# Seven half-K block products for 44 feature tiles, ahead of both branches, with narrower edge blocks in the attention

## The chip, the core and the metric

The kernel runs on one core of a Trainium2 chip. The metric is the device time of one execution in microseconds, as the median of several runs. TensorE (PE) multiplies matrices into the eight banks of PSUM, VectorE (DVE) and ScalarE (ACT) work elementwise and are the only engines here that read PSUM, GpSimd (POOL) does little, and SyncE (SP) issues nearly all transfers between device memory and the on-chip buffer from one queue, in order.

## What is computed

A hybrid encoder layer over two sequences, a prompt of 1024 tokens (s = 0) and a sample of 2048 (s = 1), each with 16 learned meta tokens ahead. All in float32.

```python
xn = _rmsnorm(h, g_pre)
proj = xn @ w_in + b_in                      # 1024 -> 6672 columns
na_q, na_k, na_v, na_z, ml_qk, ml_v, ml_z, ml_o, ml_g, mg = jnp.split(proj, SPLIT_IDX, axis=-1)
ya = _neighbourhood_attention(na_q, na_k, na_v, na_rpb)   # 8 heads of 64, windows of 8 rows x 16 columns of a 64 wide grid
ya = (ya * jax.nn.silu(na_z)) @ w_a
yb = (_mlstm_branch(ml_qk, ml_v, ml_g, ml_o, ml_conv_w, ml_head_g) * jax.nn.silu(ml_z)) @ w_b   # 4 heads of 128, both directions
ga, gb = jnp.split(jax.nn.sigmoid(mg), 2, axis=-1)
y = (ga * ya + gb * yb) @ w_out
return h + _rmsnorm(y, g_post)
```

## The kernel before

Every float32 operand of a large product is split into a rounded part (hi) and the rest (lo): ScalarE copies hi, VectorE subtracts to get lo. `mm3` then adds three products (hi hi, hi lo, lo hi) into one PSUM bank. A weight tile is loaded as `wraw`, split into `whi` and `wlo` (`wpump`, four buffers of each), and the split parts are written back to device memory for later use. The tokens are split into `xh` and `xl` (`build_half`, 512 tokens at a time).

There are two streams of work. The dense stream (`dense`) makes the projections and the final stage. A feature-major tile (`fm_half`) holds 128 columns of `proj` for 512 tokens: eight k tiles x three parts, 24 matmuls of 512 columns, into a `pj` bank, and then `fm_evac`. A token-major unit (`tm_unit`) takes 128 tokens x 256 columns. `PLAN` lists the order of the groups: sequence, first token and kinds of columns (m: for the mLSTM, n: for the attention, g: the merge gates, f: final blocks of 512 tokens, `final` and `final_out`). The sparse stream (`sparse`) makes the two branches: `ml` (gates, then for each head `ml_states` and `ml_outputs`, two chunks of 128 tokens at a time) and `na` (per head and block of eight rows, four units of 16 query columns each: `na_scores`, `na_scale`, `na_turn`, `na_out`).

`run` writes both streams into one program. The order on TensorE is as written: after each step of a branch, which names a length in microseconds (`A_D`, `A_A`, `A_NA`), dense matmuls of that length are put in. `STEPS` sets the order of the branches: mLSTM of the prompt, its attention, mLSTM of the sample, its attention. A branch starts when the groups that it needs have been written; until then the dense stream is alone. The order on the other engines is set when the program is built, by a scheduler that knows its own durations.

Names that the steps touch: `sc`, `tr` and `sm` are PSUM banks (one, two, two; `pj` has three). In `ml_outputs`, `um` is the decay tile of a pair of chunks, four buffers, loaded from `ud`; VectorE adds the mask `trim` (L1245), multiplies by the scores (L1279), and `sl` (L1286) is its last reader. `num` and `ccl` are the numerators and the low part of the state. In `na`, `prb` holds the probabilities of a unit, `pts` their transpose, `yg` the output of a head pair. `tg` are the merge gates in the final stage, `yh`, `yl`, `mh`, `mlo` its operands.

The attention's key columns: a unit reads 32 of the 64 grid columns, from `KC0`; the matmul count of a unit follows from that, a chunk of eight key columns at a time:

```python
KC0 = (0, 8, 24, 32)
    N, kc, g0 = ns * 32, KC0[cb], (5, 1, 0)[typ]
    for ch in range(4):
        nc.tensor.transpose(pt[:ks, ch, :], pr_[:, ch * ks:(ch + 1) * ks], self.ident)
```

Of the kernel before, what the change touches and what calls it, by code (L numbers as in the profile page):

```python
# [17 lines left out]
P = 128  # L18
# [3 lines left out]
NM = 16  # L22
# [18 lines left out]
PLAN = ((0, 0, "m"), (0, 0, "n"), (1, 0, "m"), (1, 1024, "m"), (1, 1024, "n"), (1, 0, "n"), (1, 0, "g"), (1, 1024, "g"), (0, 0, "g"), ("f", 0, 0), ("f", 0, 1), ("f", 1, 0), ("f", 1, 1), ("f", 1, 2), ("f", 1, 3))  # L41
STEPS = (("ml", 0, ()), ("na", 0, (0, 1)), ("ml", 1, ()), ("na", 1, (0, 1, 2, 3)))
KC0 = (0, 8, 24, 32)
OFFC = (15, 7, 7, -1)
# [27 lines left out]
def _consts():  # L72
# [9 lines left out]
    for typ, tl in ((0, 0), (1, 1), (2, R // 8 - 1)):  # L82
# [3 lines left out]
        for si, row in enumerate(slots):  # L86
            for c0 in range(49):
                m = np.full(64, NEG, np.float32)
                if row is None:
                    m[(8 if c0 < 24 else 32):][:NM] = 0.0  # L90
                else:
                    m[c0:c0 + 16] = 0.0
                masks[typ, c0, si] = m
# [27 lines left out]
class K:  # L121
# [3 lines left out]
    def __init__(self, tc, ins, outs):  # L125
# [7 lines left out]
        self.need = False  # L133
        self.hold, self.early = deque(), True
# [14 lines left out]

    def psum(self, tag, shape):  # L150
        return self.pp.tile(shape, F32, name=tag, tag=tag, bufs=BANKS[tag])

    def mm3(self, out, ah, al, bh, bl, start=True, stop=True):

        mm = self.nc.tensor.matmul
        mm(out, ah, bh, start=start, stop=False)  # L156
        mm(out, ah, bl, start=False, stop=False)  # L157
        mm(out, al, bh, start=False, stop=stop)  # L158
# [25 lines left out]
    def setup2(self):  # L184
# [5 lines left out]
        self.bq8 = cp.tile([P, 4], F32, name="bq8")  # L190
        nc.vector.tensor_scalar(self.bq8, self.bfm[:, 0:4], 0.125, None, op0=ALU.mult)
# [28 lines left out]
    def wload(self, most=2):  # L220

        while self.wreq and sum(x[1] is not None for x in self.wraw) < most:
            key, src, nk, w = self.wreq.popleft()
            raw = None
            if key not in self.wseen:
# [5 lines left out]
    def wpump(self, most=NBW, parts=1, copy=None):  # L231
# [4 lines left out]
        while self.wraw and self.wout < most:  # L236
# [4 lines left out]
            if raw is None:  # L241
# [153 lines left out]
    def build_half(self, s, t0, res):  # L395

        nc, wp = self.nc, self.wp
        if (s, t0) in self.xkept:
# [9 lines left out]
            return  # L408
        if s == 0:
# [55 lines left out]
    def xkeep(self, s, t0, x):  # L465
        where = [j for j, g in enumerate(PLAN) if g[:2] == (s, t0 // 1024 * 1024)]
        if where[-1] - where[0] >= len(where):
# [6 lines left out]
    def beside(self):  # L474

        self.turn += 1
        if self.xput and self.turn % 2:
# [3 lines left out]
    def fm_evac(self, col, s, t0, meta, chunks, ps):  # L481
# [7 lines left out]
        for (c0, c1), p in zip(chunks, ps):  # L489
# [6 lines left out]
            if col < C_NK:  # L496
                nc.scalar.activation(o.rearrange("p (b r c) -> p r b c", r=8, b=4), q.rearrange("p (r b c) -> p r b c", r=8, b=4),
                                     AF.Identity, bias=self.bq8[:, bi:bi + 1], scale=0.125)
# [22 lines left out]
        if meta and C_NK <= col < C_NV:  # L521
# [3 lines left out]
            nc.gpsimd.tensor_copy(km[:, 32:48], st[:, :NM])  # L525
# [69 lines left out]
    def tm_store(self, col, wd, s, n, cnt, tok, st):  # L595
# [30 lines left out]
        else:  # L626
            if tok is None:
                for lo in (8, 32):
# [8 lines left out]

    def layout(self, cols):

        fm = dict(m=[C_MQ + P * j for j in range(8)], n=[c + P * j for c in (C_NQ, C_NK, C_NZ) for j in range(4)],  # L640
                  g=[C_GA + P * j for j in range(16)])
# [1074 lines left out]
```

## Time and profile before

| | |
|---|---|
| median of 3 runs | 2837.75 us (2827.61 to 2838.41) |
| span of the profiled execution | 2832.5 us |
| its mean granted TensorE clock in the slices | 9 tenths or more in all 40 |
| TensorE busy | 2789.4 us, 17312 matmuls |
| VectorE busy | 1795.0 us, 4931 instructions |
| ScalarE busy | 1306.5 us, 3135 instructions |
| DMA | 655.12 MB, mean 231 GB/s |

The profiled execution has no time of its own in the list; its span is 5.25 us below the median and lies within the three runs. In the profile a busy time is the union of the instructions' spans. L12 is line 12 of the kernel. A row of a group reads: line, engine, operation, out<-in by the program's names, shape, count, busy total and mean span in ns, idle time of the engine ahead of them and what ended it. A row of a stretch reads: stretch, its length, busy us and count of each engine, granted clock, share of the DMA engines' time, GB/s.

### The profile page before, as it was taken

How to read it: one execution, taken by the hardware profiler on the slowest of the kernel's cores; microseconds unless marked ns; L12 is line 12 of the kernel's file. 1: busy time of each engine (PE TensorE's matmuls, PEld its weight loads, DVE VectorE, ACT ScalarE, POOL GpSimd, SP SyncE). 2: the span in 40 equal slices, each digit the busy share in tenths (PEclk: the TensorE clock that was granted, in tenths of full speed). 3: DMA queues.
4: the chain of work that ended last, by engine and by line, in shares of the span. 5: the costliest groups of instructions: out<-in, count | busy, mean ns of one | idle time of the engine just before them, and what ended most of it. 6: DMA issues, size and time to landing. Idle time of an engine off the chain costs nothing.

```text
span 2832.5 us, 49151 instructions
## 1 busy us (share of the span) xinstructions
PE 2789.4 (98%) x17312; PEld 2483.0 (88%) x17312; DVE 1795.0 (63%) x4931; ACT 1306.5 (46%) x3135; POOL 16.0 (1%) x103
## 2 busy tenths in 40 slices
PE   9999999999999999999999999999999999999998
PEld 7998898999899988888988888888888988989888
DVE  5232687576466654456766666474679888787854
ACT  5122556444444443355455555463455554545421
POOL 0000000000000000000000000000000000000000
PEclk9999999999999999999999999999999999999999
DMA  9554768754975554675656785556679998998965
GB/s 372 183 185 182 266 204 317 244 187 167 349 233 150 178 168 141 181 268 187 208 175 216 253 279 189 194 172 191 187 217 353 299 314 282 283 301 248 308 229 191
DMA packets 378279, 655.12 MB, mean 231 GB/s; under 512 B 50896, under 2 KB 199840, under 8 KB 378032
## 3 DMA queue, kind: packets, MB, share of 16 engines
q1 hardware_dynamic: 376912, 649.29, 69.7%
q0 software_dynamic: 1120, 2.69, 0.4%
q8 instruction: 137, 2.24, 0.3%
q14 instruction: 110, 0.90, 0.1%
HBM read 449.61 MB, written 202.22 MB: 230 GB/s over the span
## 4 chain that ended last, share of the span: by engine, by line
PE 85%; DMA 8%; DVE 5%; ACT 1%; issue 1%; SPq 0%; DVEq 0%; ACTq 0%
PE pj L156 15%; PE pj L157 15%; PE pj L158 15%; PE pj L577 7%; PE pj L578 7%; PE pj L579 7%; PE sm L887 3%; PE pj L1507 2%; PE pj L1509 2%; PE pj L1508 2%; PE tr L875 2%; DMA um<-ud 1%; PE sm L157 1%; PE sm L158 1%; DMA kr<-nk 1%; DMA yl<-yb 1%
## 5 line engine op out<-in xcount | busy, mean ns | idle before, releaser
L156 PE MATMUL pj<-xh,whi 128*128 128x512 f32 (+1 forms) x1792 | 706.5, 394 | 1.9 <-ACT whi L250 1.7
L157 PE MATMUL pj<-xl,whi 128*128 128x512 f32 (+1 forms) x1792 | 690.3, 385 | 0.4 <-DVE xl L322 0.4
L158 PE MATMUL pj<-xh,wlo 128*128 128x512 f32 (+1 forms) x1792 | 689.1, 385 | 0.3 <-DVE wlo L251 0.3
L577 PE MATMUL pj<-whi,xh 128*128 128x256 f32 (+3 forms) x1576 | 449.9, 285 | 1.5 <-ACT st L507 1.5
L578 PE MATMUL pj<-wlo,xh 128*128 128x256 f32 (+3 forms) x1576 | 444.0, 282 | 0.0
L579 PE MATMUL pj<-whi,xl 128*128 128x256 f32 (+3 forms) x1576 | 443.7, 282 | 0.0
L158 PEld LDWEIGHTS pj<-xh,wlo 128*128 128x128 f32 x1792 | 337.6, 188 | 72.2 <-DVE wlo L251 0.5
L156 PEld LDWEIGHTS pj<-xh,whi 128*128 128x128 f32 x1792 | 338.0, 189 | 62.3 <-ACT whi L250 2.6
L157 PEld LDWEIGHTS pj<-xl,whi 128*128 128x128 f32 x1792 | 338.2, 189 | 57.7 <-issue 1.0
L577 PEld LDWEIGHTS pj<-whi,xh 128*128 128x128 f32 (+1 forms) x1576 | 293.5, 186 | 3.3 <-ACT st L507 1.9
L579 PEld LDWEIGHTS pj<-whi,xl 128*128 128x128 f32 (+1 forms) x1576 | 293.3, 186 | 0.9
L578 PEld LDWEIGHTS pj<-wlo,xh 128*128 128x128 f32 (+1 forms) x1576 | 293.2, 186 | 1.0
L1507 PE MATMUL pj<-whi,mh 128*128 128x256 f32 x768 | 220.6, 287 | 2.0 <-DVE yo L1538 2.0
L1509 PE MATMUL pj<-whi,mlo 128*128 128x256 f32 x768 | 217.0, 283 | 0.0
L1508 PE MATMUL pj<-wlo,mh 128*128 128x256 f32 x768 | 217.0, 282 | 0.0
L878 DVE TENSOR_TENSOR pts<-tr,pts 96x512 fp32r<-96x512 f32 (+2 forms) x192 | 131.4, 684 | 83.8 <-ACT pts L877 82.8
L877 ACT ACTIVATE pts<-tr 96x512 fp32r<-96x512 f32 (+2 forms) x192 | 113.9, 593 | 127.1 <-PE tr L875 126.7
L156 PE MATMUL pj<-yh,whi 128*128 128x512 f32 x384 | 155.1, 404 | 3.2 <-ACT yh L1426 2.1
L158 PE MATMUL pj<-yh,wlo 128*128 128x512 f32 x384 | 152.0, 396 | 0.0
L157 PE MATMUL pj<-yl,whi 128*128 128x512 f32 x384 | 151.5, 394 | 0.2 <-DVE yl L1411 0.2
L1507 PEld LDWEIGHTS pj<-whi,mh 128*128 128x128 f32 x768 | 145.8, 190 | 3.8 <-DVE yo L1538 2.2
L1508 PEld LDWEIGHTS pj<-wlo,mh 128*128 128x128 f32 x768 | 145.9, 190 | 1.7
(278 smaller groups left out, 5014.0 us busy)
## 6 DMA issues: line engine op xcount, KB each, us to landing
whi<-wh SPq DMA_DIRECT2D x176, 512.0 KB
wlo<-wl SPq DMA_DIRECT2D x176, 512.0 KB
wraw<-wu SPq DMA_DIRECT2D x64, 512.0 KB
wh<-whi SPq DMA_DIRECT2D x64, 512.0 KB
wl<-wlo SPq DMA_DIRECT2D x64, 512.0 KB
gt<-st SPq DMA_DIRECT2D x96, 256.0 KB
tg<-gt SPq DMA_DIRECT2D x96, 256.0 KB
xt<-xt SPq DMA_DIRECT2D x32, 512.0 KB
```

The costliest lines, as they stand in the source:

```text
L156: mm(out, ah, bh, start=start, stop=False)
L157: mm(out, ah, bl, start=False, stop=False)
L158: mm(out, al, bh, start=False, stop=stop)
L577: nc.tensor.matmul(o, xh, wh, start=k == 0, stop=False)
L578: nc.tensor.matmul(o, xh, wl, start=False, stop=False)
L579: nc.tensor.matmul(o, xl, wh, start=False, stop=k == KT - 1)
L877: nc.scalar.activation(pts[:ks, :, 0, :], pt[:ks], AF.Copy)
L878: nc.vector.tensor_tensor(pts[:ks, :, 1, :], pt[:ks], pts[:ks, :, 0, :].bitcast(F32), op=ALU.subtract)
L887: nc.tensor.matmul(av[:, :256], vt[:ks, kc // 8 + ch].rearrange("p a b -> p (a b)"), pts[:ks, ch].rearrange("p a b -> p (a b)"), start=ch ...
L1507: nc.tensor.matmul(o, mh[:, k, xs], wh, start=k == 0, stop=False)
L1508: nc.tensor.matmul(o, mh[:, k, xs], wl, start=False, stop=False)
L1509: nc.tensor.matmul(o, ml[:, k, xs], wh, start=False, stop=k == KT - 1)
```

## The change

Four things are done together.

1. Strassen's scheme in Winograd's form for 44 tiles: 24 of the prompt (na_q, na_z and all 16 gate tiles) and 20 of the sample's first 1024 tokens (mLSTM q and k, na_q, na_k, na_z). A visit takes four tiles. x is cut in two token halves and two K halves, the weights in two K halves and two pairs of tiles; seven products of half the K stand for eight. The sums of x blocks are made once and kept in device memory (`prebuild`, `sstage`, `sfactor`), the sums of weight blocks per visit (`sload`, `ssum`, then split like any weight). Results are put together in PSUM and with snapshots (`ssnap`) and adds (`sadd`).
2. This stream stands alone, ahead of both branches, right after the first group. What is left is plain and is rationed among the branch steps by a new factor in `STEPS`.
3. The two edge units of a head read 24 key columns, not 32 (`KCN`).
4. The mLSTM scores of two chunks: q's two parts lie side by side (`qx`), one 256-wide product and one 128-wide replace three; their sum `ss` is made by ScalarE and VectorE before the decay is multiplied on (`weigh`). The factor 1/8 of the attention's q moves from the eviction to `na_prep`.

```diff
-PLAN = ((0, 0, "m"), (0, 0, "n"), (1, 0, "m"), (1, 1024, "m"), (1, 1024, "n"), (1, 0, "n"), (1, 0, "g"), (1, 1024, "g"), (0, 0, "g"), ("f", 0, 0), ...
-STEPS = (("ml", 0, ()), ("na", 0, (0, 1)), ("ml", 1, ()), ("na", 1, (0, 1, 2, 3)))
-KC0 = (0, 8, 24, 32)
+FIRST = (("S", ((0, 0, (C_NQ, C_NZ, C_GA, C_GA + 512, C_GA + 1024, C_GA + 1536)),
+                (1, 0, (C_MQ, C_MK, C_NQ, C_NK, C_NZ)))),)
+PLAN = ((0, 0, "akt"),) + FIRST + ((1, 0, "Gt"), (1, 1024, "akqztGh"), (1, 0, "h"), ("f", 0, 0), ...
+STEPS = (("ml", 0, (), 0.5), ("na", 0, (0, 1), 1.47), ("ml", 1, (), 0.48), ("na", 1, (0, 1, 2, 3), 0.58))
+KC0 = (0, 8, 24, 40)
+KCN = (24, 32, 32, 24)
...
+    def sorder(self, visits):
+        n = sum(len(v[2]) for v in visits)
+        out = [(0, u) for u in (1, 6, 5, 2, 7)]
+        for m in range(1, n):
+            out += [(m, 1), (m - 1, 4), (m - 1, 3), (m, 6), (m, 5), (m, 2), (m, 7)]
+        return out + [(n - 1, 4), (n - 1, 3)]
...
+    def ssum(self, n, u):
+        b, sub = self.sb[n], lambda *x: self.behind(self.nc.vector.tensor_tensor(*x, op=ALU.subtract))
+        if u == 6:
+            sub(b[0, 0], b[0, 1], b[0, 0])
+            b["t"] = self.s0.tile([P, 2, 512], F32, name="t2", bufs=1)
+            sub(b["t"], b[1, 1], b[0, 0])
+        elif u == 7:
+            sub(b[0, 1], b[1, 1], b[0, 1])
+        elif u == 4:
+            sub(b["t"], b[1, 0], b["t"])
+        return {1: b[0, 0], 6: b.get("t"), 5: b[0, 0], 2: b.get((1, 0)), 7: b[0, 1], 4: b.get("t"), 3: b.get((1, 1))}[u]
...
+    def ssnap(self, p, col):
+        x = self.wp.tile([P, 2, WU], F32, name="sn", tag="stT", bufs=4).rearrange("p a c -> p (a c)")[:, :512]
+        self.nc.scalar.activation(x, p, AF.Identity, bias=self.scol(col))
+        return x
...
+        if u == 1:
+            q["p", a] = self.ssnap(q["C", a], c0)
+        elif u == 6:
+            q["u", a] = self.ssnap(q["C", a], c1)
+        elif u == 7:
+            q["w", a] = self.ssnap(q["C", a], c1)
+        elif u == 2:
+            self.sadd(q["A", a], q["p", a], c0, s, t0)
+        elif u == 4:
+            self.sdirect(q["C", a], c0, s, t0 + 512)
+        elif u == 3:
+            self.sadd(q["B", a], q["u", a], c1, s, t0)
...
+    def sstream(self, visits, nxt):
...
+                for k in range(4):
+                    self.mm3(p, w[0][:, a, k], w[1][:, a, k], xh[:, k], xl[:, k], start=k == 0 and u in (1, 5, 2), stop=k == 3, skip_group_check=True)
...
-        N, kc, g0 = ns * 32, KC0[cb], (5, 1, 0)[typ]
+        kc, kn, g0 = KC0[cb], KCN[cb], (5, 1, 0)[typ]
+        N, nb = ns * kn, kn // 8
...
-        for ch in range(4):
+        for ch in range(nb):
             nc.tensor.transpose(pt[:ks, ch, :], pr_[:, ch * ks:(ch + 1) * ks], self.ident)
...
-                self.mm3(s0[:, j * P:(j + 1) * P], kh[:, j, :], kl[:, j, :], qh[:, j, :], ql[:, j, :])
+                nc.tensor.matmul(s0[:, j].rearrange("p a t -> p (a t)"), kh[:, j, :], qx[:, j].rearrange("p a t -> p (a t)"),
+                                 start=True, stop=False)
+                nc.tensor.matmul(s0[:, j, 0], kl[:, j, :], qx[:, j, 0], start=False, stop=True)
+            ss = mp.tile([P, CB, P], F32, name="ss", bufs=1)
+            nc.scalar.activation(ss, s0[:, :, 1], AF.Copy)
+            nc.vector.tensor_tensor(ss, ss, s0[:, :, 0], op=ALU.add)
...
-            acc += w
+            acc += w * self.rate
```

How the order changes, at three places. First TensorE at the mLSTM scores of the sample; `tr` and `sm` rows are the outputs of the pair before. Before:

```order
L156 MATMUL sc<-qh,kh 128x128
L157 MATMUL sc<-ql,kh 128x128
L158 MATMUL sc<-qh,kl 128x128
L1391 MATMUL tr<-ident,hb 128x128 x4
L156 MATMUL pj<-xh,whi 128x512
L157 MATMUL pj<-xl,whi 128x512
L158 MATMUL pj<-xh,wlo 128x512
L156 MATMUL pj<-xh,whi 128x512
L157 MATMUL pj<-xl,whi 128x512
L158 MATMUL pj<-xh,wlo 128x512
L156 MATMUL tr<-cch,qh 128x260
```

And after:

```order
L1602 MATMUL sc<-qx,kh 128x256
L1604 MATMUL sc<-qx,kl 128x128
L1602 MATMUL sc<-qx,kh 128x256
L1604 MATMUL sc<-qx,kl 128x128
L1724 MATMUL tr<-ident,hb 128x128 x4
L165 MATMUL tr<-cch,qx 128x260
L166 MATMUL tr<-ccl,qx 128x260
L167 MATMUL tr<-cch,qx 128x260
```

The two triples of dense matmuls between the scores and the output products are gone here; between the first and the last mLSTM matmul of the sample stand 1308 dense matmuls of 512 columns, where there were 2460.

Second, TensorE in the sample's attention. Before, a unit's scores, transposes and output products have six dense matmuls of a projection between them:

```order
L850 MATMUL sc<-kd,stk 128x384
L851 MATMUL sc<-kx_23205,qB_23203 128x384
L156 MATMUL pj<-xh,whi 128x512
L157 MATMUL pj<-xl,whi 128x512
L158 MATMUL pj<-xh,wlo 128x512
L156 MATMUL pj<-xh,whi 128x512
L157 MATMUL pj<-xl,whi 128x512
L158 MATMUL pj<-xh,wlo 128x512
L875 MATMUL tr<-ident,prb 96x128 x4
```

After, an edge unit's scores are followed at once by another unit's transposes, and the dense matmuls are those of a final block:

```order
L1178 MATMUL sc<-kd,stk 128x288
L1179 MATMUL sc<-kx_24672,qB_24670 128x288
L1203 MATMUL tr<-ident,prb 96x128 x4
L165 MATMUL pj<-yh,whi 128x512
L166 MATMUL pj<-yl,whi 128x512
L167 MATMUL pj<-yh,wlo 128x512
L165 MATMUL pj<-yh,whi 128x512
L166 MATMUL pj<-yl,whi 128x512
L167 MATMUL pj<-yh,wlo 128x512
L1215 MATMUL sm<-pts,vt 128x256 x4
```

The units have moved together, and an edge unit has 288 columns where it had 384.

Third, VectorE beside the dense tiles of the prompt. Before, evictions (`pj`, times the token's norm) and weight splits alternate:

```order
L495 TENSOR_TENSOR pj<-pj,rr 128x248
L495 TENSOR_TENSOR pj<-pj,rr 128x264
L495 TENSOR_TENSOR pj<-pj,rr 128x512
L251 TENSOR_TENSOR wlo<-wraw,whi 128x1024
L495 TENSOR_TENSOR pj<-pj,rr 128x512
```

After, in the product stream (`b_` and `t_` are weight blocks and their sums, `sn` the snapshots, `st` the results):

```order
L831 TENSOR_TENSOR st<-sm,sn 128x512
L790 TENSOR_TENSOR b_4786<-b_4892,b_4786 128x1024
L831 TENSOR_TENSOR st<-sm,sn 128x512
L253 TENSOR_TENSOR wlo<-b_4786,whi 128x1024
L253 TENSOR_TENSOR wlo<-b_5044,whi 128x1024
L790 TENSOR_TENSOR t_4966<-b_4970,t_4966 128x1024
L253 TENSOR_TENSOR wlo<-t_4966,whi 128x1024
L831 TENSOR_TENSOR st<-tr,sn 128x512 x2
L253 TENSOR_TENSOR wlo<-b_4892,whi 128x1024
```

Block sums have come between the splits, and the evictions add a snapshot to a bank.

381 lines of the change are left out of this document (320 added, 61 removed).

## The prediction

> **What bounds the kernel now.** I read the page first: the totals of each engine and the 40 slices.
>
> ```profile
> span 2832.5 us, 49151 instructions
> PE 2789.4 (98%) x17312; PEld 2483.0 (88%) x17312; DVE 1795.0 (63%) x4931; ACT 1306.5 (46%) x3135; POOL 16.0 (1%) x103
> ...
> PE   9999999999999999999999999999999999999998
> ...
> DVE  5232687576466654456766666474679888787854
> ...
> PEclk9999999999999999999999999999999999999999
> DMA  9554768754975554675656785556679998998965
> ```
>
> TensorE is busy in every slice at full clock: the time is its matmuls. VectorE is the second engine and is close to full only in the last quarter. Next the busy time of each stage; the cuts are where the mLSTM branch or the attention branch begins beside the dense work.
>
> ```profile
> core 0: us, PE busy (x) PEld busy (x) DVE busy (x) ACT busy (x) POOL busy (x), PEclk, DMA share, GB/s
> 0.00:268.00 268.00, 262.84 (x1891) 244.23 (x1891) 95.01 (x203) 80.61 (x129) 1.67 (x27) 1.00 0.67 241
> 268.00:740.00 472.00, 471.68 (x3177) 429.55 (x3176) 320.52 (x988) 236.83 (x595) 6.39 (x34) 1.00 0.69 233
> 740.00:1141.00 401.00, 401.00 (x2596) 364.95 (x2595) 228.96 (x573) 172.90 (x373) 1.80 (x16) 1.00 0.61 191
> 1141.00:1941.00 800.00, 792.44 (x4313) 676.69 (x4312) 497.45 (x1616) 407.52 (x1068) 4.08 (x22) 1.00 0.64 209
> 1941.00:2727.00 786.00, 767.02 (x4750) 682.58 (x4750) 603.30 (x1420) 394.85 (x927) 2.05 (x4) 1.00 0.85 270
> 2727.00:2832.00 105.00, 94.41 (x596) 85.01 (x594) 49.73 (x132) 13.81 (x44) 0.00 (x0) 0.96 0.65 236
> ```
>
> The rows are: first projections; mLSTM of the prompt; its attention; mLSTM of the sample; its attention; the last block. In the two mLSTM stages VectorE has 68% and 62% of the time to do, in the sample's attention 77%. That room is what the change uses up.
>
> Third, what one matmul costs. A busy span overlaps the next one, so I take start to start, from the timeline on TensorE (start, span, line, shape).
>
> ```profile
> 1000.21 0.39 PE L156 MATMUL pj<-xh,whi 128*128 128x512 f32 x1
> 1000.44 0.39 PE L157 MATMUL pj<-xl,whi 128*128 128x512 f32 x1
> ...
> 1000.90 0.35 PE L850 MATMUL sc<-kd,stk 128*128 128x416 f32 x1
> 1001.09 0.36 PE L851 MATMUL sc<-kx,qB 128*128 128x416 f32 x1
> ...
> 1301.40 0.22 PE L156 MATMUL sc<-qh,kh 128*128 128x128 f32 x1
> ...
> 1302.02 0.44 PE L156 MATMUL pj<-xh,whi 128*128 128x512 f32 x1
> ...
> 2600.66 0.64 PE L887 MATMUL sm<-pts,vt 104*128 104x256 f32 x4
> 2601.14 0.28 PE L1507 MATMUL pj<-whi,mh 128*128 128x256 f32 x1
> ...
> 2604.38 0.60 PE L875 MATMUL tr<-ident,prb 128*104 128x128 f32 x4
> 2604.74 0.37 PE L1507 MATMUL pj<-whi,mh 128*128 128x256 f32 x1
> ```
>
> 512 columns step by 0.23 us (0.233 over longer runs), 416 by 0.19, 256 by 0.12 (four in 0.48), a transpose by 0.09 (four in 0.36), and the six 128-wide score products of the mLSTM take 0.62 together. All stepped matmuls of the old program at these prices make 2761 us; the other 71 of the span are the start, the end and waits.
>
> **What the matmuls lose.** (1) A visit treats four feature tiles x 1024 tokens. Plain, it needs 4 tiles x 2 token halves x 8 k x 3 parts = 192 matmuls of 512 columns; as seven half-K products, 7 x 2 x 4 x 3 = 168. Eleven visits save 264: 264 x 0.2335 = 61.6 us. (2) Both edge blocks of every attention head read 24 key columns, not 32: 96 of 192 units. Each loses one transpose and one output product: 96 x (0.09 + 0.12) = 20.2 us. Their two score products shrink by 128, 104 or 96 columns (32 units each): 64 x 328 columns x 0.455 ns (0.233 / 512) = 9.6 us. (3) The mLSTM scores take a 256-wide and a 128-wide product in place of three 128-wide: 48 pairs of chunks x (0.62 - 2 x (0.12 + 0.10)) = 8.6 us. Together 100 us: 2832.5 - 100 = 2732 if nothing else changed.
>
> **Where the matmuls now stand.** The order of the new program, priced so, sums to 2659 us, in these stages: first group and product stream 777; prompt mLSTM 259; prompt attention 499; sample mLSTM 430; sample attention 478; tail 151; between stages 65. Before, the same five stages had 256, 461, 373, 772, 739, then 94 and 66. The stream takes dense work away from under the branches: the sample mLSTM stage has 2406 matmuls where it had 4184 (1308 of 512 columns for 2460), the sample attention 3258 for 4652. The branches' own VectorE, ScalarE and DMA work is the same, so it must fit into 0.56 and 0.65 of the time.
>
> **VectorE by stage.** A busy span has a tail that the next instruction covers when the queue is full (timeline of VectorE):
>
> ```profile
> 486.62 0.69 DVE L1373 SCALAR_TENSOR_TENSOR hb<-tog,hb 128x512 f32<-128x512 f32 x1
> 487.22 1.22 DVE L460 TENSOR_TENSOR xl<-xt,xh 128x1024 fp32r<-128x1024 f32 x1
> ```
>
> Span 0.69, step 0.60: about 0.085 us per instruction is covered. So each demand has an upper end (busy time) and a lower one (spans less tails); I take the lower, since a full queue is the case in question. Groups of instructions (busy total, mean ns, idle time before them), first over the span, the last row over the sample's mLSTM stage alone:
>
> ```profile
> L250 ACT ACTIVATE whi<-wraw 128x1024 fp32r<-128x1024 f32 x61 | 64.4, 1057 | 96.7 <-PE pj L157 48.7 <-PE pj L579 45.8 <-DMA wraw<-wu 1.9
> ...
> L251 DVE TENSOR_TENSOR wlo<-wraw,whi 128x1024 fp32r<-128x1024 f32 x61 | 74.5, 1221 | 27.3 <-ACT whi L250 27.1
> ...
> L495 DVE TENSOR_TENSOR pj<-pj,rr 128x512 f32<-128x512 f32 x59 | 40.8, 695 | 71.8 <-PE pj L158 68.0 <-ACT rr L308 3.5
> ...
> L1279 DVE TENSOR_TENSOR um<-um,sc 128x256 f32<-128x256 f32 x96 | 36.0, 412 | 36.7 <-PE sc L158 36.5
> ...
> L1245 DVE TENSOR_TENSOR um<-um,trim 128x256 f32<-128x256 f32 x64 | 26.5, 424 | 81.4 <-DMA um<-ud 81.4
> ```
>
> - Sample mLSTM: 497 busy, of which I estimate 59 as dense (16 weight splits of 1.22, the x splits, evictions of 0.70 and less). The branch keeps 438, gains 32 adds (ss) of 0.41 = 13, and about 50 of new neighbours (final blocks, splits): 501, or 455 with tails covered. TensorE has 430. On top comes a wait that costs nothing today: VectorE stands 81 us for the decay tile um, whose buffer it frees itself two chunk pairs earlier (sl, in order), then a DMA refills it. By the two orders and these prices the VectorE work between the freeing and the next add (L1245) grows from about 1.4 to 2.5 us; the 81 us are 1.27 per add, so I leave 35. 490, and 2% for ScalarE: 500. Bounds 430 and 455 + 81 = 536.
> - Prompt mLSTM: 320 less about 95 dense, plus 7 and 28: 260, or 235 with tails covered, and some 16 of um: 251 for TensorE's 259. The gate chain at its start has half its cover. Loss 21, bounds 5 and 35.
> - Sample attention: 603 less 12 (narrow units) less about 105 of final-block work now elsewhere: 486, or 460. TensorE 478. DMA is busy 0.85 of 786 = 668; the bytes issued from here to the end fall from 233 to 187 MB, and the longer tail has more of them: about 480. Three engines level.
> - Prompt attention: 229 less 6, with more evictions beside it: below 250 against 499. It stays TensorE's.
> - Stream: per visit four block sums and seven splits of 1.22, six adds out of PSUM of 0.70: 17.6 us of VectorE beside 168 x 0.2335 = 39.2 of TensorE. Were it not covered: a product's chain (sum 1.22, hi about 1.06, lo 1.22 = 3.5 us) still fits into its 5.6 us. Scaling x and its block sums (about 70 us in all) hide there too, and SP's transfers: 2 MB of blocks in and 2 MB of results out per visit, 107 GB/s. On SP a load of b12 waits for product 7's split and holds the stores behind it, for one product at most; four st buffers cover that. POOL's queue keeps its 103 instructions.
>
> How the chip behaved with full queues:
>
> ```profile
> 480.00:500.00 20.00, 20.00 (x105) 16.88 (x104) 19.92 (x57) 13.68 (x31) 0.10 (x1) 1.00 1.00 350
> ...
> 2160.00:2200.00 40.00, 37.76 (x246) 33.61 (x245) 38.37 (x80) 26.95 (x60) 0.00 (x0) 1.00 1.02 347
> 2680.00:2727.00 47.00, 45.05 (x362) 45.02 (x363) 26.03 (x68) 19.88 (x63) 0.00 (x0) 0.96 0.45 155
> ```
>
> At 99.6% busy VectorE delayed nothing for 20 us; at 96%, with DMA full, TensorE kept 94%. What TensorE waits for now (total, times, longest) is the same two engines:
>
> ```profile
> PE sm L850 <- DVE yg L893: 7.5, 5, 2.1
> PE sm L887 <- ACT prb L858: 3.8, 3, 2.1
> PE sm L157 <- DVE vl L1256: 3.1, 2, 1.7
> ```
>
> So sample attention 478 / 0.94 = 508, loss 30; bounds 488 and 541 (VectorE's 460 at 85%). Others: start 12 as now (268 against 256), stream 4 (0 to 60), prompt attention 5, tail 12, between 1. Sum: 2659 + 70 + 21 + 30 + 12 + 4 + 5 + 12 + 1 = 2814 for the span. The shown median is 5 above the profiled span (2837.75 against 2832.5), so **2819 us**, 0.7% faster: of 100 us saved, 81 come back as waits, most of them for VectorE.
>
> **A rule that speaks against it.** The rows of 2680 and 2727 show a granted clock of 0.96 where TensorE had 45.05 of 47 and 94.41 of 105 us to do, while 2160 kept 1.00. The Trainium skill, TensorE: Matmul & The Clock Gate, section "A second HAM failure mode: psum-queue depth-cycling", says that short idles between groups of matmuls can make the clock swing between half and full rate. The trace agrees that idling costs clock, by 4%, and shows no half rate here. By the rows the three squeezed stages (259 + 430 + 478 us) would lose 4%, 47 us, which is rival D below; by the page each of their groups could step at up to twice its price for a while.
>
> **Rivals.**
> - A, VectorE keeps up: waits stay at the 71 us of now: 2732 + 5 = 2737. For it: the 480 row. Against: 455 and more against 430.
> - B, slower: VectorE's wait for um stays what it is, since a refill takes its time whatever is queued ahead, and now every microsecond of it is TensorE's: 455 + 81 = 536, with 5% for ScalarE (407 busy now, less about 90 of dense work, plus 45: 84% of 430), 564: 2819 + 64 = 2883. It decides from 54 us of um waits upwards (stage 519 us: the old time). For it: the L1245 row; against: the longer queue ahead of the add.
> - C, the seven products don't come cheaper: three or four products share a PSUM bank (snap by ScalarE, then accumulate on) and four weight buffers feed them; at 0.8 us of wait for each of 77 products 62 us are gone: 2819 + 58 = 2877. Against: products on one bank are at least two (11 us) apart.
> - D, the clock: if the 1167 us of the three squeezed stages ran at 0.96, 47 us more: 2866.
>
> **Chances.** Forecast 0.48, A 0.18, B 0.20, C 0.08, D 0.06. Half a percent (14 us) is what a measurement of this kernel tells from no change. The forecast's own range is 2785 to 2852: 0.32 of its 0.48 lie under 2823.5, 0.15 within the half percent, 0.01 above. With A, faster has 0.50. B gives 0.17 slower and 0.03 same, C 0.05 and 0.03, D 0.03 and 0.03: slower 0.26, same 0.24. The range 2745 to 2880 reaches nearly to A's and B's values and leaves out their outer halves.
>
> **What would show it.** Right: TensorE busy over 99% of the stream; in the sample mLSTM stage VectorE busy over 95% and TensorE waiting for what VectorE makes (ss, um, sl, ccl, num), the stage 480 to 520 us long; VectorE's idle time before the add of trim there between 25 and 45 us; sample attention 495 to 525. A is right if TensorE stays over 98% in both; B if the idle time before that add is 60 us or more; C if the stream shows TensorE waiting for whi, wlo or sn; D by the clock of the rows. The forecast is wrong above all if the 455 is mis-sized.

## The result, and the profile after

The changed kernel takes 3035.8 us in the median of four runs, the kernel before 2832.93 beside it: the ratio is 1.0717, 95% interval 1.0695 to 1.0739. The forecast was 2819 us, 0.7% faster. The profiled execution has a span of 3030.7 us (its time is 3032.45). First the page: totals and the slices of three rows.

```profile
span 3030.7 us, 48697 instructions
PE 2770.0 (91%) x16760; PEld 2445.8 (81%) x16760; DVE 1954.4 (64%) x5161; ACT 1400.9 (46%) x3296; POOL 16.2 (1%) x103
...
PE   8999999999788989999999789797868888889998
...
DVE  4423565644477883444555488877987888788844
...
PEclk9999999999899999999999999998989999999999
```

TensorE has 552 matmuls fewer, but its busy time fell by only 19 us and it now stands idle for 261 of 3030.7 us (43 before). The stretches of the changed kernel, cut as in the prediction: first group; product stream; mLSTM of the prompt; its attention; mLSTM of the sample; its attention; tail.

```profile
core 0: us, PE busy (x) PEld busy (x) DVE busy (x) ACT busy (x) POOL busy (x), PEclk, DMA share, GB/s
0.00:340.00 340.00, 331.47 (x2481) 312.89 (x2482) 132.49 (x243) 85.65 (x131) 2.74 (x23) 0.99 0.71 257
340.00:774.00 434.00, 431.57 (x1860) 349.01 (x1859) 250.50 (x279) 194.17 (x249) 0.21 (x2) 1.00 0.53 180
774.00:1144.00 370.00, 310.77 (x2193) 289.19 (x2192) 265.09 (x908) 195.38 (x545) 5.24 (x36) 0.94 0.62 201
1144.00:1699.00 555.00, 549.43 (x3443) 492.92 (x3441) 260.94 (x638) 202.45 (x423) 1.81 (x16) 1.00 0.57 181
1699.00:2285.00 586.00, 475.29 (x2437) 394.49 (x2438) 481.78 (x1632) 373.62 (x1045) 4.11 (x22) 0.91 0.65 208
2285.00:2874.00 589.00, 523.06 (x3340) 469.71 (x3339) 495.96 (x1299) 323.07 (x821) 2.05 (x4) 0.95 0.85 256
2874.00:3030.00 156.00, 148.41 (x1015) 137.63 (x1014) 67.62 (x165) 26.60 (x83) 0.00 (x0) 0.98 0.68 243
```

The stream is as clean as forecast (431.57 of 434 us busy, clock 1.00), and so is the prompt's attention. From the first to the last instruction of each branch in the timeline the stages last 364, 541, 582 and 589 us. Against the priced sum of 2659 the span lost some 371 us: 105 in the prompt's mLSTM, 152 in the sample's, 111 in its attention, 3 everywhere else. The prices, though, cut the stages by TensorE's own order, from a branch's first matmul to its last, and so cut the losses are 74, 147 and 100 us, 28 ahead of the first mLSTM matmul and 23 elsewhere. The difference is at the seam behind the stream: GpSimd clears the first tiles of the prompt's mLSTM at 774.2 us, but TensorE still has 48 matmuls of the stream and 42 of a projection to do there (21 us by the prices), and then waits for the gate chain (`g_lf`):

```profile
804.64 1.07 PE L1266 MATMUL sm<-g_lf,tri 128*128 128x36 f32 x4 [9.29 <-DVE g_lf L1260]
```

In the three stages neither engine is full: VectorE 72, 82 and 84%, TensorE 84, 81 and 89%. What TensorE waits for in the whole span (total, times, longest), and below it the largest waits of VectorE in the sample's mLSTM:

```profile
PE tr L1724 <- DVE hb L1719: 56.6, 8, 13.0
PE sm L1215 <- ACT prb L1186: 22.5, 8, 6.1
PE sm L1266 <- DVE g_lf L1260: 19.8, 2, 10.5
PE sm L1215 <- DVE yg L1221: 14.0, 6, 6.4
PE sm L167 <- DVE ktl L1483: 12.4, 20, 2.2
```

```profile
DVE um L1573 <- DMA um<-ud: 44.8, 36, 3.4
DVE g_lf L1249 <- DMA g_t<-gg: 12.8, 1, 12.8
DVE yl L1744 <- ACT yh L1759: 6.2, 6, 3.7
```

hb is a normalised head of the mLSTM, whose transposes stand in TensorE's order at a fixed place. VectorE is late with it, and behind that many short waits follow. The chain of waits in this stage names the transfer of um oftenest (17% of it).

### The profile page after: what moved, and what is told of

It is laid out like the page before. It is cut to its first block, busy times and chain, and to the rows that moved or that the text cites. A ratio compares the mean times of both kernels' runs of the same rounds, so it can differ in the third digit from the quotient of the medians.

```text
span 3030.7 us, 48697 instructions
## 1 busy us (share of the span) xinstructions
PE 2770.0 (91%) x16760; PEld 2445.8 (81%) x16760; DVE 1954.4 (64%) x5161; ACT 1400.9 (46%) x3296; POOL 16.2 (1%) x103
## 4 chain that ended last, share of the span: by engine, by line
PE 39%; DMA 16%; DVE 13%; ACT 4%; issue 2%; SPq 0%; DVEq 0%; ACTq 0%
PE pj L165 6%; PE pj L166 6%; PE pj L167 6%; DMA um<-ud 5%; PE pj L607 3%; PE pj L608 3%; PE pj L609 3%; PE pj L1840 2%; PE pj L1842 2%; PE pj L1841 2%; PE sm L1215 2%; DMA kr<-nkm 1%; PE tr L1203 1%; DMA va<-mv 1%; DMA yl<-yb 1%
## 5 line engine op out<-in xcount | busy, mean ns | idle before, releaser
L165 PE MATMUL pj<-xh,whi 128*128 128x512 f32 (+1 forms) x1224 | 484.9, 396 | 9.7 <-ACT st L537 5.7
L166 PE MATMUL pj<-xl,whi 128*128 128x512 f32 (+1 forms) x1224 | 471.4, 385 | 0.2 <-DVE xl L335 0.2
L167 PE MATMUL pj<-xh,wlo 128*128 128x512 f32 (+1 forms) x1224 | 470.4, 384 | 0.1
L165 PEld LDWEIGHTS pj<-xh,whi 128*128 128x128 f32 x1224 | 235.2, 192 | 49.7 <-ACT st L537 6.7
L167 PEld LDWEIGHTS pj<-xh,wlo 128*128 128x128 f32 x1224 | 234.5, 192 | 48.2 <-DVE wlo L264 0.3
L166 PEld LDWEIGHTS pj<-xl,whi 128*128 128x128 f32 x1224 | 235.4, 192 | 36.8 <-issue 0.5
L1205 ACT ACTIVATE pts<-tr 96x384 fp32r<-96x384 f32 (+2 forms) x192 | 103.6, 540 | 150.0 <-PE tr L1203 149.5
L1206 DVE TENSOR_TENSOR pts<-tr,pts 96x384 fp32r<-96x384 f32 (+2 forms) x192 | 118.4, 617 | 81.1 <-ACT pts L1205 80.7
L1215 PE MATMUL sm<-pts,vt 96*128 96x256 f32 (+2 forms) x672 | 121.1, 297 | 43.0 <-ACT prb L1186 22.5
```

The source lines that it names most:

```text
L165: mm(out, ah, bh, start=start, stop=False, **more)
L166: mm(out, ah, bl, start=False, stop=False, **more)
L167: mm(out, al, bh, start=False, stop=stop, **more)
L1205: nc.scalar.activation(pts[:ks, :nb, 0, :], pt[:ks, :nb], AF.Copy)
L1206: nc.vector.tensor_tensor(pts[:ks, :nb, 1, :], pt[:ks, :nb], pts[:ks, :nb, 0, :].bitcast(F32), op=ALU.subtract)
L1215: nc.tensor.matmul(av[:, :256], vt[:ks, kc // 8 + ch].rearrange("p a b -> p (a b)"), pts[:ks, ch].rearrange("p a b -> p (a b)"), start=ch ...
```

## Experiments

All times are medians; the ratios are to the kernel before, run on the same chip.

| run | what differs | us | ratio (95%) |
|---|---|---|---|
| plain_stream | change, plain products | 3072.1 | 1.0835 (1.0795 to 1.0874) |
| pe_extra | change, +86 us of TensorE work | 3070.4 | 1.0829 (1.0773 to 1.0884) |
| dve_extra | change, +63 us of VectorE work, mLSTM | 3099.5 | 1.0934 (1.0899 to 1.0969) |
| dve_extra_na | change, +102 us of VectorE work, attention | 3079.3 | 1.0869 (1.0802 to 1.0936) |
| um_noload | change, um not loaded | 2979.7 | 1.0509 (1.0459 to 1.0558) |
| um_six | change, six um buffers | 3041.0 | 1.0727 (1.0693 to 1.0762) |
| um_pinned | change, add of trim held back | 3006.4 | 1.0611 (1.0537 to 1.0686) |
| norm_later | change, transposes of hb 4 steps later | 3009.4 | 1.0613 (1.0572 to 1.0655) |
| later_start | change, 60 us dense ahead of mLSTM | 3022.4 | 1.0668 (1.0600 to 1.0736) |
| mended | um_pinned, norm_later and later_start together | 2976.8 | 1.0507 (1.0424 to 1.0589) |
| prompt_visits | change with the prompt's six visits alone, nearly the old order | 2935.4 | 1.0365 (1.0334 to 1.0395) |
| prompt_visits_um | the same, um from GpSimd's queue, later transposes | 2939.1 | 1.0369 (1.0345 to 1.0393) |
| even_cover | change, even order | 2938.1 | 1.0350 (1.0297 to 1.0402) |
| even_cover_um | the same, six um, later transposes | 2916.9 | 1.0288 (1.0265 to 1.0311) |
| even_mended | even order with slightly lower rates, and the three mends | 2883.8 | 1.0195 (1.0169 to 1.0222) |
| edges_only | before and part 3 | 2802.8 | 0.9890 (0.9868 to 0.9912) |
| edges_scores | before and parts 3 and 4 | 2801.1 | 0.9886 (0.9866 to 0.9907) |
| edges_pinned | before, part 3, add of trim held back | 2789.7 | 0.9852 (0.9837 to 0.9867) |

**The products, and the order.** Theory: the loss is in the stages behind the stream. Rival: the seven products cost time of their own.

```diff
-PLAN = ((0, 0, "akt"),) + FIRST + ((1, 0, "Gt"), ...
+PLAN = ((0, 0, "akt"), (0, 0, "qzGh"), (1, 0, "akqz"), (1, 0, "Gt"), ...
```

> The changed kernel with the 44 tiles in the same place and order but as plain products of the whole K: 264 matmuls of 512 columns more, 61.6 us by the prices. If the seven products are as cheap as priced and the loss lies wholly in the stages behind them: 3036 + 62 = 3098 us, and against the kernel before +265 us for the new order alone. If the seven products cost time of their own (rival C): 3036 to 3050.

36 us between the medians (41 between the profiled executions), not 62. With plain products the first matmul of the prompt's mLSTM comes 49 us later, with no wait for `g_lf` ahead of it:

```profile
853.23 0.53 PE L1262 MATMUL sm<-g_lf,tri 128*128 128x36 f32 x4
```

From its first to its last matmul that mLSTM then takes 322 us, against 333 in the change. The rest is equal within 6 us a stage. So the products brought most of their price, and 21 to 26 us of it are lost where the stream meets the mLSTM, 9.3 of them in the wait for the gate chain.

The order alone is what costs. Beside plain_stream stands edges_scores, the last but one of the table: the old order, plain products, parts 3 and 4. Both have 17024 matmuls, and in the slower one VectorE has no more to do and the transfers move no more (634.10 MB for 655.07). First edges_scores (span 2800.3 us), then plain_stream (3071.7):

```profile
PE 2752.4 (98%) x17024; PEld 2446.3 (87%) x17024; DVE 1781.7 (64%) x4979; ACT 1299.9 (46%) x3183; POOL 16.5 (1%) x103
```

```profile
PE 2837.1 (92%) x17024; PEld 2500.6 (81%) x17024; DVE 1744.2 (57%) x4962; ACT 1285.0 (42%) x3167; POOL 15.9 (1%) x103
```

The new order of the same work costs 271 us: TensorE is idle for 187 us more, and its matmuls are busy for 85 us more. So the 203 us between the two kernels are about 32 off for parts 3 and 4, 271 on for the order and 36 off for the seven products.

**Which engine's time counts.** Work that changes no result was added to one engine at a time.

```diff
+            if k == 0 and self.done and self.rate < 1.0 and not self.tail:
+                for _ in range(4):
+                    self.nc.tensor.matmul(ps[q][:, :c1 - c0], w[0][:, k, :], x[0][:, k, c0:c1], start=True, stop=True)
...
                 nc.vector.tensor_tensor(sl[:, d], um, sh[:, d].bitcast(F32), op=ALU.subtract)
+                nc.vector.tensor_tensor(sl[:, d], um, sh[:, d].bitcast(F32), op=ALU.subtract)
+                nc.vector.tensor_tensor(sl[:, d], um, sh[:, d].bitcast(F32), op=ALU.subtract)
...
         nc.vector.tensor_tensor(pts[:ks, :nb, 1, :], pt[:ks, :nb], pts[:ks, :nb, 0, :].bitcast(F32), op=ALU.subtract)
+        nc.vector.tensor_tensor(pts[:ks, :nb, 1, :], pt[:ks, :nb], pts[:ks, :nb, 0, :].bitcast(F32), op=ALU.subtract)
```

The first edit is pe_extra, the second dve_extra, the third dve_extra_na.

> The changed kernel with 86 us of additional TensorE work in the squeezed stages, by the prices of the prediction: the first product of a tile is repeated (four times in a projection, two times in the final blocks), 6 us in the prompt's mLSTM, 51 in the sample's mLSTM, 28 in its attention; the results do not change. If TensorE's time there is the bound (at a lower clock), 3036 + 86 = 3122 us or more. If VectorE and the transfers set the pace and TensorE only waits (116 and 66 us in the two stages), the added work fills its waits: 3036 to 3060. If the low clock comes from the idling (rival D) and matters, a busier TensorE gets a higher clock and the time stays or falls: 3000 to 3036, granted clock of the two stages back above 0.97.

> The changed kernel with the subtraction that makes sl done three times (the same result): 128 more VectorE instructions in the sample's mLSTM and 64 in the prompt's, 0.33 us each by step, 42 + 21 = 63 us. If VectorE's work sets these stages: 3036 + 63 = 3099 us. If the two engines share the path, as the 86 us of TensorE work that cost 35 say: a half, 3065. If VectorE has room where it waits for um: 3040.

> The changed kernel with the subtraction that makes the low part of pts done twice (the same result): 128 more VectorE instructions in the sample's attention and 64 in the prompt's, about 0.53 us each by step: 68 and 34 us. The prompt's attention is TensorE's (VectorE 47%) and should take nothing in any theory. If VectorE's work sets the sample's attention as it does the mLSTM: 3036 + 68 = 3104 us. If VectorE and TensorE share the path: about 3070. If the transfers (0.85 of the stage) or TensorE's clock set it: 3036 to 3050.

TensorE's 51 us in the sample's mLSTM made the stage 26 longer (608), its 28 in the attention 15 (604), its 6 in the prompt's mLSTM nothing. VectorE's 42 in the sample's mLSTM made it 43 longer (625), its 21 in the prompt's 10, its 68 in the sample's attention 43 (632), its 34 in the prompt's attention 1 us (12 of dve_extra's 64 fell in the sample's attention, which the edit does not touch). These are stages of one profiled execution each; for pe_extra the medians give 35 us in all for the 86 added, the profiled executions 43. Here is the sample's mLSTM of pe_extra and of dve_extra, then dve_extra_na's two attentions:

```profile
1700.00:2308.00 608.00, 523.17 (x2636) 432.71 (x2637) 482.20 (x1630) 373.38 (x1041) 4.09 (x22) 0.93 0.63 200
```

```profile
1712.00:2336.00 624.00, 488.61 (x2419) 402.97 (x2420) 521.68 (x1758) 374.34 (x1041) 4.09 (x22) 0.88 0.61 195
```

```profile
1142.00:1683.00 541.00, 541.00 (x3408) 486.45 (x3407) 296.95 (x699) 201.00 (x421) 1.02 (x2) 1.00 0.57 178
...
2288.00:2920.00 632.00, 536.00 (x3336) 474.98 (x3335) 562.38 (x1427) 322.91 (x821) 2.04 (x4) 0.94 0.80 238
```

VectorE has 39.9 us more to do in dve_extra's row, and the stage is longer by as much: TensorE is idle for 25 us more of it, and the same matmuls are busy for 13 us more, at a granted clock of 0.88 for 0.91. So VectorE sets the sample's mLSTM, at 82% busy; TensorE's time counts about half; in the sample's attention both count, 0.63 (VectorE) and 0.54 (TensorE) of what is added; in the prompt's attention VectorE's work is free. The DMA engines, 0.85 busy in the sample's attention, were not varied by themselves.

**The refill of um (rival B).**

```diff
-                    nc.sync.dma_start(um, src)
-                nc.vector.tensor_tensor(um, um, self.trim[:, d], op=ALU.add)
+                nc.vector.tensor_tensor(um, self.trim[:, d], self.trim[:, d], op=ALU.add)
...
+                    um = mp.tile([P, CB, P], F32, name="um", bufs=6)
...
+                self.behind(nc.vector.tensor_tensor(um, um, self.trim[:, d], op=ALU.add))
```

In this order: um_noload, um_six, um_pinned. `behind` keeps an instruction behind the one written before it on its engine.

> The changed kernel without the transfers of the decay tile um (its add reads the mask twice, so the decays are not the reference's); every instruction on the engines stays. VectorE stood 44.8 us before this add in the sample's mLSTM and 23.3 us in the prompt's. If the refill is what holds these stages (rival B), both waits go and their time with them: 3036 - 68 = 2968 us or less, the sample's mLSTM stage from 582 to about 535. If the two in-order queues hold each other up in many places (the lockstep theory), the next wait takes over most of it: 3010 to 3030. If VectorE's own work were the bound, nothing but the 68 us of idle would go either, so that this run tells the refill from the lockstep and not from the work.

> The changed kernel with six buffers for um, not four, so that a refill starts a pair of chunks earlier; the memory comes from the st buffers (three, not four). With no load at all 56 us went. If two more buffers take the refill off the path: 2980 to 2995 us, of which the missing st buffer may take some back in the stream. If the transfer is late for its place in SP's queue: 3020 to 3036.

> The changed kernel with the add of trim to um held behind the VectorE instruction written before it, so that the order of VectorE no longer puts it right behind the expected landing of the transfer. If the wait is a matter of the add's place, most of the 68 us go: 2980 to 3000 us. If VectorE only does later what it must do anyway and the exponentials come late: 3030 or slower.

Without the load 56 us go, 38 in the sample's mLSTM and 23 in the prompt's (4 came back in the sample's attention): nearly all of the 44.8 + 23.3. That wait was on the path. Yet six buffers change nothing. The waits of VectorE in um_six, then the add in um_pinned:

```profile
DVE um L1573 <- DMA um<-ud: 67.4, 47, 3.8
```

```profile
L1573 DVE TENSOR_TENSOR um<-um,trim x96: 390/420/430, 849.8 to 2209.7; 128x256 f32<-128x256 f32 x96
...
  DMA um<-ud: 37.3, 24
```

In the timeline the transfer is issued 0.1 us (median) after its buffer is freed in the change, and some 10 us earlier than that with six buffers; but in both the add starts 4.0 and 4.2 us (medians in the sample's mLSTM) after the issue. VectorE's order, set when the program is built, had moved the add up along with the transfer, away from the multiplication that needs it (by the medians 28 us ahead of it, where it was 14). That the scheduler placed it by the landing it expected is a guess. Held back, with four buffers, the add stands 11.7 us behind the issue, 31 us of the wait go and 29 us of the time. This kernel's stages: 347 and 560 us.

**Two more places: the transposes of hb, and the seam.**

```diff
-        for _ in range(12):
+        for _ in range(16):
...
-("na", 0, (0, 1), 1.47)
+("na", 0, (0, 1), 1.26)
...
+                x = 60.0 if w == ("m", 0, 0) else 0.0
+                while x > 0.0:
+                    x -= next(dense)
```

> The changed kernel with the transposes of the normalised heads four branch steps later (16, not 12, after the scaling). TensorE stands 56.6 us ahead of these transposes for hb. If they simply stand too early in TensorE's order, each of the 24 gets about 6 us more and most of the wait goes: 3036 - 35 = 3000 us. If VectorE is late with everything there (lockstep, or the refill of um), TensorE waits at the next thing instead: 3026 to 3036.

> The changed kernel with 60 us of plain dense work between the end of the product stream and the start of the prompt's mLSTM, and that much less beside the prompt's attention (rate 1.26 for 1.47); the priced sum stays. If the 41 us are the stream's late transfers, at full DMA, ahead of the gate chain's, the dense work covers them: 2996 to 3010 us. If it is the thin cover of the gate chain itself: 3030 to 3036.

> The changed kernel with the pinned add, the norm's transposes four steps later and the later start. If the three terms add up: 3036 - 50 - 27 - 35 = 2924 us. If they are the same wait seen three times: 2960 or more. In either case slower than the kernel before, since VectorE's work in the sample's mLSTM and the sample's attention stay as they are.

Later transposes took 26 us off, but only 2 in the sample's mLSTM: its wait for hb fell from 43.1 to 20.1 us, that for qx rose from 8.1 to 20.1. The wait moved on, as behind an engine that is late in general. The rest came in parts of 10 us and less elsewhere. The dense work at the seam took the wait for `g_lf` away and 13 us off, of the 21 to 26 lost there; what holds the rest is open. (The 41 us of its expectation had the seam begin at 774 us.) The three together gave 59 us, for 69 one by one: mostly separate causes, none of them large.

**The cover.** If the thin and uneven cover is the cause, the loss must fall as the same work gets more TensorE time beside it.

```diff
-PLAN = ((0, 0, "akt"),) + FIRST + ((1, 0, "Gt"), (1, 1024, "akqztGh"), (1, 0, "h"), ...
+PLAN = ((0, 0, "akt"),) + FIRST + ((1, 0, "Gu"), (1, 1024, "au"), (1, 1024, "kqzv"), (1, 0, "vh"), (1, 1024, "Gh"), ...
+STEPS = (("ml", 0, (), 0.58), ("na", 0, (0, 1), 0.80), ("ml", 1, (), 0.70), ("na", 1, (0, 1, 2, 3), 0.75))
```

u are the mLSTM's units of t, v the attention's. prompt_visits has FIRST with the prompt's visit alone and the groups (1, 0, "au"), (1, 1024, "au"), (1, 1024, "kqzv"), (1, 0, "kqzv"), (1, 0, "Gh"), (1, 1024, "Gh").

> The changed kernel, all four parts and all 77 products, with another order of the plain groups and other rates: the projections that the sample's mLSTM does not need are written behind its start, so that the four stages get 291, 304, 572 and 575 us of TensorE work by the prices where the change has 258, 499, 430 and 478. The priced sum stays 2659. VectorE's estimated work (235, 245, 455, 460) is then 80% of each stage, where it was 91, 49, 106 and 96%. If the loss is the uneven, thin cover, the stages lose about a tenth each: 2659 + 50 for the start, the seams and the tail + 174 = 2880 us. If the stream or its seam is at fault, or any stage under 85% of VectorE is as good as another: 3000 or more in the first case, 2760 in the second.

> As even_cover, with six um buffers (three of st) and the norm's transposes four steps later. In the changed kernel these were worth up to 56 and 27 us. With more cover VectorE's wait is on the path for less of its time: 20 to 50 us below even_cover; nothing, if at 80% the waits are hidden already.

> The seven-product stream for the prompt's 24 tiles alone (six visits), the sample's 20 tiles plain and beside the branches, the old order of groups behind it, and rates (0.75, 0.93, 0.82, 1.0) that give the four stages 359, 342, 649 and 603 us of TensorE work by the prices, where the changed kernel has 258, 499, 430 and 478; parts 3 and 4 as in the change. Priced sum 2687 against 2659 for the change and 2761 for the kernel before. If the loss is the thin cover (VectorE's work is then about 72% of each stage, not 94% to 106% of the TensorE work): losses near the 71 us of before, 2687 + 71 + 30 = 2790 us, faster than both. If the stream itself or any thinner cover costs as much as it saves: 2830 or more.

> As prompt_visits, with the norm's transposes four steps later and the transfers of um issued from GpSimd's queue, which is nearly empty, in place of SP's. If the refill waits behind other transfers on SP, VectorE's wait before the add falls by half or more, and with a thicker cover this is worth less than in the changed kernel: 0 to 20 us below prompt_visits. If the refill takes its time from the freeing of the buffer on, nothing changes: within 5 us of it.

> The seven-product kernel with the even order (even_cover, 2938 us), the pinned add, the later transposes and 60 us of dense work ahead of the prompt's mLSTM (three mends that took 59 us off the changed kernel). If they add up here too: 2938 - 59 = 2880 us; if the evener cover had already taken half of what they mend: 2910. In both cases above the 2833 of before; 2833 or less would say that thin cover is not what keeps it above.

The even order gave back 98 us, not the 156 expected. The sample's mLSTM in even_cover and in prompt_visits, then the latter's sample attention:

```profile
1503.00:2147.00 644.00, 597.59 (x3384) 515.04 (x3385) 481.48 (x1634) 378.51 (x1048) 4.09 (x22) 0.96 0.68 221
```

```profile
1403.00:2091.50 688.50, 665.74 (x3527) 562.80 (x3528) 474.84 (x1605) 389.36 (x1064) 4.09 (x22) 0.98 0.67 213
2100.00:2828.50 728.50, 651.10 (x4099) 584.19 (x4097) 568.57 (x1409) 362.68 (x898) 2.04 (x4) 0.94 0.86 271
```

For the same mLSTM, TensorE's priced work, what the stage lost beyond it and VectorE's busy share go together: before, 772 us, loss 19 to 28, 62%; prompt_visits 649, 39, 69%; even_cover 572, 72, 75%; the change 430, 152, 82%. The prompt's mLSTM goes the same way, less steeply (by TensorE's order and in the same order of kernels 461 us, loss 6; 359, 42; 291, 60; 259, 74). The sample's attention does not: 739 us, loss 27; 603, 115; 575, 100; 478, 100, with VectorE 77, 78, 79 and 84% busy. Nor does VectorE's share decide by itself, for in 600 us of the kernel before, within that attention, it was 83% busy beside a TensorE at 97% and full clock:

```profile
2080.00:2680.00 600.00, 582.97 (x3701) 521.43 (x3699) 498.86 (x1166) 313.99 (x736) 2.05 (x4) 1.00 0.93 297
```

One difference stands out, and no run separates it: in this stage of the kernel before some 600 dense matmuls were projections, in that of the other three at most 44, and the rest belong to final blocks, whose operands VectorE and ScalarE must make first. My 2880 and 2790 took the loss at 80 and 72% too low, and prompt_visits lost 125 us in the sample's attention (728 for 603), at least 24.7 of them because its final blocks were reached before the attention had made their input: TensorE waited that long for yh, in two pieces. GpSimd's queue for um, together with later transposes, left the time where it was (the wait for um fell from 123 to 106 us). With the three mends the even order comes to 2883.8 us, 54 below even_cover, and stays 1.95% above the kernel before.

**Parts 3 and 4 alone, and the best kernel.**

> The kernel before with part 3 alone, the 24-column edge units; order, plain products and mLSTM scores as before. By the prices 20.2 + 9.6 = 29.8 us less TensorE work in stages where VectorE stays below 80%. If covered TensorE time comes off one for one: 2835 - 30 = 2805 us. If the attention stages are held by something else already: 2820 to 2835.

> The kernel before with parts 3 and 4 (edge units and mLSTM scores), without the product stream and with the old order. Prices: 29.8 + 8.6 = 38.4 us less TensorE work, 48 more adds of 0.41 us on VectorE and as many copies on ScalarE. If the cover hides these: 2835 - 38 = 2797 us. If the longer way from the scores to the weights (copy, add, then the multiplication) stalls TensorE: no better than the edge units alone.

> The kernel before with the 24-column edge units and the pinned add of trim, which took 30 us off the changed kernel. If idle time of VectorE is free while the dense work covers it: the same as the edge units alone, 2795 to 2808 us. If the wait cost something there too: 2770 to 2790.

The edge units bring what was priced: 29.8 us expected, 1.10% or 31 us measured (28 between the medians). The shorter scores took 6.2 us off TensorE's busy time (2758.6 to 2752.4) and 1.8 off the time, which the intervals do not tell from nothing. The pinned add, kept beside the full cover, gave about 11 us more, the second of the two cases expected (the two intervals only just miss each other): with TensorE 99% busy most of VectorE's wait was hidden, not all, as 37 us less of it (101.7 to 64.7) were worth 11. This is the fastest kernel of the study:

```profile
span 2787.5 us, 48730 instructions
...
PE 2753.5 (99%) x17120; PEld 2452.7 (88%) x17120; DVE 1764.9 (63%) x4931; ACT 1289.7 (46%) x3135; POOL 16.1 (1%) x103
```

## Why the prediction was wrong

- **What held.** The prompt's attention with the time between stages took 564 us for 564, the tail 157 for 151. Rival C's waits are not in the stream, where TensorE was busy for 431.57 of 434 us; what the products lost they lost behind it, at the seam. The edge units' price holds (edges_only). The 774 us of the first two rows look like the 777 priced, but by TensorE's order the first mLSTM matmul came at 804.6, 28 us late where 16 were forecast.
- **The step that failed** is the loss of the three squeezed stages: in the sum 70 us for the sample's mLSTM, 21 for the prompt's and 30 for the sample's attention. Measured by TensorE's order, as they were priced, they are 147, 74 and 100: 200 us more than forecast, while the other terms, 34 us in the forecast, came to 51. (By the branches' own first and last instructions it is 152, 105 and 111, and 3.) What they stand for, the price of the new order, is shown by plain_stream and edges_scores: 271 us for the same matmuls.
- **Inside it, the sample's mLSTM.** I took 455 us of VectorE work (tails covered), left 35 for um and 2% for ScalarE: 500. Measured: 481.8 busy, between the two ends of 455 and 501, and about 104 idle, of which um 44.8 (25 to 45 were forecast), the gate chain's load 12.8, and some 47 in waits of a few us or less, for which the sum had no term. The row of 480 to 500, where VectorE was 99.6% busy, was 20 us in which its queue never ran dry; over this stage, in which TensorE and VectorE feed each other in fixed orders, VectorE reached 82% (over 95% was forecast). That it sets the stage, as forecast, is shown by dve_extra; that TensorE would wait only for VectorE's excess is what fell, since half of TensorE's own work counts too.
- **Prompt's mLSTM.** I gave 21 us and no seam. 21 to 26 us around its start appear only behind the seven products; 13 went with 60 us of dense work ahead.
- **Sample's attention.** "478 / 0.94" took the rate of 40 us for that of 589. dve_extra_na and pe_extra show both engines on the path, each in part. Why it lost 100 us here and 27 in the kernel before stays open: neither more cover nor a lower share of VectorE brought it down.
- **Rival B** was right in kind: the um wait was on the path almost one for one. It was not its size that decided: 44.8 us, below the 54 that I named, and without it the kernel is still 5.1% slower.
- **Rival D.** The clock fell to 0.94, 0.91 and 0.95 in these stages. The timeline of TensorE in the change shows how (start, span, line, shape, idle before):

```profile
1814.38 1.09 PE L1724 MATMUL tr<-ident,hb 128*128 128x128 f32 x4 [9.01 <-DVE hb L1719]
...
1816.12 0.63 PE L167 MATMUL pj<-xh,wlo 128*128 128x512 f32 x1
1816.55 0.63 PE L165 MATMUL pj<-xh,whi 128*128 128x512 f32 x1
...
1820.71 0.40 PE L165 MATMUL pj<-xh,whi 128*128 128x512 f32 x1
1820.95 0.40 PE L166 MATMUL pj<-xl,whi 128*128 128x512 f32 x1
```

After 9 us of waiting a step of 512 columns takes 0.43 us, and 0.24 again 6.3 us after the wait ended. The prediction read the rows of the kernel before as showing no half rate. They are averages: its timeline has the same steps of 0.43 us in the very stretch of 2727 to 2832, from 2738.1 to 2741.1, behind a wait of 2.14 us:

```profile
2736.28 0.49 PE L156 MATMUL pj<-yh,whi 128*128 128x512 f32 x1 [2.14 <-ACT yh L1426]
...
2738.11 0.63 PE L158 MATMUL pj<-yh,wlo 128*128 128x512 f32 x1
2738.53 0.63 PE L156 MATMUL pj<-yh,whi 128*128 128x512 f32 x1
```

The Trainium skill, TensorE: Matmul & The Clock Gate, section "What's actually happening", puts the array at half rate after an idle window of about 3.4 us, and at full rate after as long a busy one. The traces agree in kind and not in length: a wait of 2.14 us was enough in the kernel before, and behind the wait of 9 us it took nearer six than 3.4 us of work before the full rate was back. What the clock costs by itself no run separates: the slow steps come behind waits, TensorE's time counts about half in the sample's stages, and pe_extra, with fewer waits, had 0.93 for 0.91 in the sample's mLSTM and was slower. The new order's own 85 us of busier TensorE for the same 17024 matmuls hold all its slower steps, and also overlap that was lost. So slow steps are by themselves at most about 85 of the 271 us, an estimate from the two profiles, and the other 187 are idle time.

## What to carry to other kernels

Matmuls that run beside another engine's work are its cover: before pricing a saving in them, price how much of the other engine's time, waits included, they hide, and do not take for a stage the busy share that this engine reached over 20 good microseconds. The order that moved 44 tiles of cover away cost 271 us, far more than the 62 us priced for the cheaper products, while cutting matmuls in place (the edge units) paid in full. When VectorE waits for a transfer, look first at where its order puts the reader behind the issue, since more buffers may move both.

## What was not expected of the chip

- Half-rate steps came and went within single stages, in both kernels: 0.43 us a step behind a wait of 9 us, and also behind one of 2.14 us, and the full rate was back within some six microseconds of the wait's end. A mean clock of 0.96 hides them.
- Two engines can both count without either being full: in the sample's mLSTM, with VectorE 82% and TensorE 81% busy, an added microsecond cost about 1.0 on VectorE and 0.5 on TensorE.
- Six buffers in place of four left a wait of 67 us where it was (68), while a later place in the order halved it (37) and gave 29 us.
